# Group norm of a delta-rule head pair by sums and broadcast operands; one visit for the tiled output products, transposes six products later

## The chip, the cores and the metric

The kernel runs on one core of a Trainium2 chip, in one launch. The metric is the device time of that core in microseconds (us). The core's engines work side by side, each through its own list of instructions: TensorE (PE; its weight loads are shown apart as PEld), VectorE (DVE), ScalarE (ACT), GpSimd (POOL) and SyncE (SP, which here issues DMAs).

## The reference

One layer of a hybrid decoder trunk, for 512 tokens and 2048 channels, in float32:

```python
h = rms_norm(x, norm_g)
z = h @ w_in              # r, k, v, two low-rank inputs | gate | pool input | pool gate
r, k, v, wd, ad = token_shift_and_lerp(z[..., :3200])
decay = exp(-exp(-softplus(-(w0 + tanh(wd) @ w_up)) - 0.5))
a = sigmoid(a0 + ad @ a_up)
kk = normalized(k * k_k);  k = k * (1 + (a - 1) * k_a)
# per head of 64 channels, over time:
#   S = S * w_t + (S @ -kk_t) (kk_t * a_t)^T + v_t k_t^T ;  y_t = S @ r_t
y = wkv7_scan(r, decay, k, v, kk, a)
# head_group_norm: over the 64 channels of a head, at each position
yn = (y - mean(y)) * rsqrt(mean((y - mean(y))**2) + 64e-5)
y_rwkv = (yn * ln_w + ln_b + bonus) * silu(gate)
y_pool = causal_multiscale_pool(u) @ w_pool * pool_scale * silu(pool_gate)
x = x + concat(y_rwkv, y_pool) @ w_out
x = x + sigmoid(x @ w_pg + b_pg) * (p @ w_ple)
out = rms_norm(x, final_g)
```

The 16 heads are worked on in eight pairs, j = 0 to 7, of 128 channels each. The change concerns the last products of y and the group norm.

## The kernel before

**Dense products.** Each large matrix is split into a high and a low part, and a product is three matmuls (`mm3`: high by high, high by low, low by high) of 128 by 512 elements. The splits of the weights are made on the fly by ScalarE (line 132, the high part) and VectorE (line 133, the low part). A generator (`stream`) gives out the products with w_in for the coming pairs (names zr, zk, zv, zg), and those of the pool groups (zb, pp) and of the layer embedding (pple), in the order of a list. `pump(n)` issues the next n matmuls of it. These calls stand between the steps of the recurrence, so that TensorE has dense work while another engine makes the next operand.

**The recurrence of a pair** (`recur`) goes through eight chunks of 64 tokens. Per chunk TensorE has three small products in a chain: py (the state, sbd, by r and by k), which VectorE adds to mv for zs; pu (the inverted triangular factor x1 by zs), which ScalarE copies to uv; and ps (bkn by uv), from which VectorE makes the next state sbd. Six, nine and nine dense matmuls stand behind these three (`HC`). In chunk 0 `between()` issues the score products of the next pair (pm, by `scores`), whose results VectorE masks; during the later chunks VectorE also inverts the next pair's 32 by 32 blocks (`invert`, lines 657 and 661).

**The tiled products.** An output of a chunk has two parts: py, from the state, and the masked scores of the chunk (mt) by uv. The second are products with 128 rows, 64 columns and 64 moving columns, two heads per chunk; they add to the same PSUM tile, which holds four chunks. After chunk 3 and after chunk 7 TensorE makes eight such products in a row (in float32, two passes each, so 16 instructions), and ScalarE copies the tile into ysb with two instructions (line 827). A PSUM tile py has the tag "y" with two buffers, which it shares with half of the score tiles pm and with pv.

**The group norm** follows on VectorE: for each of the eight groups in a row of ysb (four times two heads) one bn_stats, one bn_aggr and one scaling (lines 842, 844, 851), and for all eight a reciprocal root by an integer guess and three Newton steps (`rsqrt`, lines 142 to 151).

**After the recurrence** `gather(j + 1)` prepares the next pair: the decay and rate products pu and pa, which ScalarE reads for sig and tha (lines 532 and 547); transposes of v (pv, copied to uv) and of the keys (pbk, two PSUM tiles, copied to bkn); H4 = 8 dense matmuls; the key norm (pss); H5 = 13 dense matmuls; then the pending `finish` of the pair before, which transposes the normed ysb into pyt, scales it on ScalarE (yo, line 860), adds the bonus and multiplies by the gate on VectorE (lines 861 and 862) and stores it; then HX = 13 dense matmuls; then the products of the blockwise inversion (pq, pmv, px), whose result ScalarE copies to x1 (line 745). For the last pair there is no `gather`; 40 dense matmuls (`HE`) stand before its `finish`. The PSUM tiles of tag "m" (pu, pa, pbk, pss, pyt, pq, pmv, px, pp) share three buffers.

**What sets the order.** TensorE's instructions keep the order in which the program emits them (`tc.keep_in_program_order`). The instructions of the other engines are put into an order at compile time by a planner, with priorities by their place in the program, and with `high_priority` and `issue_after` at the recurrence's critical ones. On the chip each engine follows its list.

Of the kernel before, what the change touches and what calls it, by code (L numbers as in the profile page):

```python
# [9 lines left out]
F32 = mybir.dt.float32  # L10
F32R = mybir.dt.float32r
I32 = mybir.dt.int32
AF = mybir.ActivationFunctionType
ALU = mybir.AluOpType

P = 128
T = 512
# [6 lines left out]
C = 64  # L24
NCH = T // C
# [9 lines left out]
def trunk_kernel(ctx: ExitStack, tc: tile.TileContext, x, p, norm_g, w_in, mu, w0, w_up, a0, a_up,  # L35
                 k_k, k_a, r_k, ln_w, ln_b, w_pool, pool_scale, w_out, w_ple, w_pg, b_pg, final_g, out):
    nc = tc.nc
    PSUM = bass.MemoryType.PSUM
    x, p, w_in, w_out, w_ple, w_pg = x[0], p[0, 0], w_in[0], w_out[0], w_ple[0], w_pg[0]
# [116 lines left out]
    def mm(*a, **k):  # L156
        i = nc.tensor.matmul(*a, **k)  # L157
        return tc.keep_in_program_order(i) if pin[0] else i

    def tr(*a):  # L160
        i = nc.tensor.transpose(*a)
        return tc.keep_in_program_order(i) if pin[0] else i
# [44 lines left out]
    for kind, nm, j in jobs:  # L207
# [7 lines left out]
        else:  # L215
            g, i = j // 4, j % 2
# [79 lines left out]
    for d in range(KT):  # L296
        xt_half(0, d)
        if d in WPOS:
            c = len(wl_)
# [41 lines left out]
    rw = s2a.enter_context(tc.tile_pool(name="rw", bufs=1))  # L341
    psS = s2a.enter_context(tc.tile_pool(name="psS", bufs=1, space=PSUM))
    psY = s2a.enter_context(tc.tile_pool(name="psY", bufs=2, space=PSUM))
# [148 lines left out]
    def pump(n):  # L492
        debt[0] += n
        while debt[0] > 0:
            c = next(big, None)
            if c is None:
                debt[0] = 0
                return
            debt[0] -= c
# [17 lines left out]
    H1, H2, H3, H4, H5, HE = 6, 12, 20, 8, 13, 40  # L517
# [36 lines left out]
    def prepare_key(j):  # L554
        k_ = need("k", j)
        kk = rw.tile([P, T], F32, name=f"kk{j}", tag="kk")
        nc.scalar.activation(kk, k_, AF.Square, scale=pc("k_k", j))
        kqh = rw.tile([P, T], F32R, name=f"kqh{j}", tag="t", bufs=4)
        kql = rw.tile([P, T], F32R, name=f"kql{j}", tag="t", bufs=4)
        split(kqh, kql, kk)  # L560
        kks[j] = (kk, kqh, kql)
# [116 lines left out]
    def gather(j):  # L678
        d = st_[j]
        bk, v_, mt = d.pop("bk"), d.pop("v_"), d["mt"]  # L680
        if j + 1 < NJ:
            prepare_key(j + 1)
            decay_and_rate(j + 1)

        uv = rw.tile([P, NCH, P], F32, name=f"uv{j}", tag="uv")
        ps = psY.tile([P, T], F32, name=f"pv{j}", tag="y")
        for tt in range(NT):
            tr(ps[:, tt * P:(tt + 1) * P], v_[:, tt * P:(tt + 1) * P], ident)
        pv = ps.rearrange("p (t c) -> p t c", c=P)
        nc.scalar.copy(uv[0:64, 0::2, :], pv[0:64])  # L690
        nc.scalar.copy(uv[64:128, 1::2, :], pv[64:128])


        bkn = rw.tile([P, NCH, P], F32, name=f"bkn{j}", tag="bkn")
        for hf in range(2):
            ps = psM.tile([P, T], F32, name=f"pbk{j}_{hf}", tag="m")
            for i in range(4):
                ch = 4 * hf + i
                tr(ps[:, i * P:(i + 1) * P], bk[:, ch // 2, 2 * (ch % 2):2 * (ch % 2) + 2, :], ident)
            nc.scalar.copy(bkn[:, 4 * hf:4 * hf + 4, :], ps.rearrange("p (c n) -> p c n", n=P))  # L700

        pump(H4)

        d.update(uv=uv, bkn=bkn)
        if j + 1 < NJ:
            norm_key(j + 1)
        pump(H5)
        if pending:
            pending.pop()()
        pump(HX)  # L710

        x1 = d["x1"]

        def units(fn):
            for u in range(8):
                for par in range(2):
                    fn(u, par, 64 * (1 - par))

        y1 = rw.tile([P, 8, 32], F32, name=f"y1{j}", tag="tm")

        with tc.issue_after(late[0].ins):
            for pb in (0, 64):
                yt = nc.vector.transpose(y1[pb:pb + 32], x1[pb:pb + 32, :, 0:32])
        if j + 1 < NJ:
            with tc.issue_after(yt.ins):
                scale_key(j + 1)
        ps3 = psM.tile([P, 8, 32], F32, name=f"pq2{j}", tag="m")
        units(lambda u, par, pb: mm(ps3[pb + 32:pb + 64, u, :],
                                                  mt[pb:pb + 32, par, u, 1 - par, 32:64],
                                                  y1[pb:pb + 32, u, :], start=True, stop=True,  # L730
                                                  tile_position=(pb, pb + 32)))
        q2t = rw.tile([P, 8, 32], F32, name=f"q2{j}", tag="xw")
        with tc.high_priority(offset=HP):
            for pb in (0, 64):
                nc.scalar.copy(q2t[pb + 32:pb + 64], ps3[pb + 32:pb + 64])
        psv = psM.tile([P, 8, C], F32, name=f"pmv{j}", tag="m")
        units(lambda u, par, pb: mm(psv[pb:pb + 64, u, :], mt[64 - pb:128 - pb, par, u, 1 - par, :],
                                    uv[64 - pb:128 - pb, 2 * (u // 2) + par, 64 * (u % 2):64 * (u % 2) + 64],
                                    start=True, stop=True))
        ps4 = psM.tile([P, 8, 32], F32, name=f"px2{j}", tag="m")  # L740
        units(lambda u, par, pb: mm(ps4[pb:pb + 32, u, :], q2t[pb + 32:pb + 64, u, :],
                                                  x1[pb + 32:pb + 64, u, 32:64], start=True, stop=True,
                                                  tile_position=(pb + 32, pb)))
        for pb in (0, 64):
            nc.scalar.copy(x1[pb:pb + 32, :, 32:64], ps4[pb:pb + 32])
        mv = rw.tile([P, 4, P], F32, name=f"mv{j}", tag="mv")
        nc.scalar.copy(zsp[0][64:128, :].rearrange("p (h t) -> p h t", h=2), psv[64:128, 0:2, :])
        nc.scalar.copy(mv.rearrange("p q (h t) -> p (q h) t", h=2), psv)
        d["mv"] = mv
        pump(2 * H1)  # L750


    def recur(j, work, between):
        d = st_.pop(j)
        pw, ar, mt, bv, uv, bkn, mv, x1 = (d[n_] for n_ in ("pw", "ar", "mt", "bv", "uv", "bkn", "mv", "x1"))
# [11 lines left out]


        ysb = rw.tile([P, NT, P], F32, name=f"ysb{j}", tag="t", bufs=4)
        py = None  # L770
        for ch in range(NCH):
            par, q = ch % 2, ch // 2
            pb = 64 * (1 - par)
# [1 line left out]
            pcc = pw[:, ch, C:C + 1]  # L775
            sl = slice((ch % 4) * P, (ch % 4 + 1) * P)
            if ch % 4 == 0:
                py = psY.tile([P, T], F32, name=f"py{j}_{ch}", tag="y")
            zs = zsp[par]
            if ch > 0:  # L780
                mm(py[:, sl], ar[:, q, 2 * par:2 * par + 2, :], cur, start=ch in (1, 4), stop=True,
                                 skip_group_check=True)
# [14 lines left out]
            if ch < NCH - 1:  # L797
# [12 lines left out]
                if ch < NCH - 2:  # L810
                    for h in range(2):
                        hc = slice(64 * h, 64 * h + 64)
                        nc.gpsimd.tensor_scalar(s0p[hc, :], nxt[hc, hc], pcn[hc], None, ALU.mult)  # L813
            if ch % 4 == 3:
                for qq in range(2):
                    for h in range(2):
                        for pr in range(2):
                            c_ = ch - 3 + 2 * qq + pr
                            yr = slice(64 * pr, 64 * pr + 64)
                            o_ = (2 * qq + pr) * P + 64 * h  # L820
                            mm(py[yr, o_:o_ + 64], mt[:, pr, 2 * (c_ // 2) + h, pr, :],
                                             uv[:, c_, 64 * h:64 * h + 64], start=False, stop=True,
                                             skip_group_check=True)
                py4 = py.rearrange("p (s c) -> p s c", c=P)
                for pr in range(2):
                    yr = slice(64 * pr, 64 * pr + 64)
                    nc.scalar.copy(ysb[yr, q - 1:q + 1, :], py4[yr, pr::2, :])
            step()
            if ch == 0:
                between()  # L830
# [4 lines left out]
            pass  # L835


        st = rw.tile([P, 8, 6], F32, name=f"st{j}", tag="st")
        mvr = rw.tile([P, 8, 2], F32, name=f"mvr{j}", tag="mvr")
        y8 = ysb.rearrange("p q (h c) -> p (q h) c", h=2)  # L840
        for i in range(8):
            nc.vector.bn_stats(st[:, i, :], y8[:, i, :])
        for i in range(8):
            nc.vector.bn_aggr(mvr[:, i, :], st[:, i, :])
        rs8 = rw.tile([P, 8, 1], F32, name=f"rs8{j}", tag="rs8")
        ve8 = rw.tile([P, 8, 1], F32, name=f"ve8{j}", tag="ve8")
        nc.vector.tensor_scalar(ve8, mvr[:, :, 1:2], 64e-5, None, ALU.add)
        nt8 = rw.tile([P, 8, 1], F32, name=f"nt8{j}", tag="nt8")
        rsqrt(rs8, ve8, nt8)
        for i in range(8):  # L850
            nc.vector.tensor_scalar(y8[:, i, :], y8[:, i, :], mvr[:, i, 0:1], rs8[:, i, :],
                                    ALU.subtract, ALU.mult)

        def finish():
            sg = need("g", j)
# [11 lines left out]
    HC, HT, HX = (6, 9, 9), 130, 13  # L867
# [13 lines left out]
    for _ in invert(0):  # L881
        pass
    pump(HT)
    gather(0)
    for j in range(NJ):
        def between():
# [291 lines left out]
```

## Time and profile before

| | |
|---|---|
| median of three runs | 1094.54 us (1093.39 to 1097.44) |
| the profiled execution | 1094.06 us, of which the profile's span is 1092.3 us |
| granted TensorE clock | 0.998 |
| busy: PE, PEld, DVE, ACT, POOL | 1067.4, 879.1, 707.9, 448.2, 74.4 us |
| tiled products (py<-uv,mt) | 256 instructions in 16 visits, 155.7 to 699.5 us |
| bn_stats, bn_aggr, scaling | 64 each; 11.0, 6.1, 15.4 us busy |

In the profile, a row of a timeline gives start, duration, engine, line, operation, and out<-in by the names of the program; a time in brackets is idle time before it, with what ended it. Rows merge equal neighbours (x16). A row of waits gives who waited for whom, then the total in us, how many times, and the longest. A row of a group gives shapes, count, busy time in us and mean ns of one, and then the idle time before them. L157 is the matmul helper, L161 the transpose helper, L132 and L133 the split of weights. Matmuls are pipelined, so that the start of the next one tells more than the duration.

### The profile page before, as it was taken

To read this page: it belongs to the slowest core of one execution; us is meant where nothing else is said; L and a number is where in the kernel's file an instruction comes from. 1 tells how busy PE (TensorE), PEld (TensorE's weight loads), DVE (VectorE), ACT (ScalarE), POOL (GpSimd) and SP (SyncE) were. 2 spreads that over 40 slices of the span, in tenths; PEclk is the share of its full clock that TensorE was granted. 3 is DMA by queue.
4 is the path that set the end of the run, shared out by engine and by line. 5 is a ranking of instruction groups with operands and counts; after the bars stand their busy time and mean duration, and the time that the engine had idled before them with its cause. 6 is when DMAs were issued, how large, how long until landed. Compare 5 with 4: busy or idle time off the path is not lost.

```text
span 1092.3 us, 17194 instructions
## 1 busy us (share of the span) xinstructions
PE 1067.4 (98%) x6060; PEld 879.1 (80%) x6060; DVE 707.9 (65%) x1835; ACT 448.2 (41%) x917; POOL 74.4 (7%) x180
## 2 busy tenths in 40 slices
PE   5999999999999999999999999999999999999996
PEld 4888878888888888787888788888888888888885
DVE  6687867878779679678886956454433424445366
ACT  7633534435335335353443344544222222233337
POOL 2100010110110110100101101000000000000000
PEclk9999999999999999999999999999999999999999
DMA  7433433332423333333334242774534438454534
GB/s 233 116 97 97 112 92 79 102 101 72 127 81 102 105 91 89 95 83 90 94 93 120 79 138 94 231 242 163 171 123 141 164 97 261 129 187 147 174 105 154
DMA packets 178485, 138.56 MB, mean 127 GB/s; under 512 B 34677, under 2 KB 139742, under 8 KB 178398
## 3 DMA queue, kind: packets, MB, share of 16 engines
q1 hardware_dynamic: 157694, 103.89, 32.2%
q10 hardware_dynamic: 20704, 33.56, 9.5%
q8 instruction: 48, 0.79, 0.3%
q14 instruction: 39, 0.32, 0.1%
HBM read 118.02 MB, written 18.87 MB: 125 GB/s over the span
## 4 chain that ended last, share of the span: by engine, by line
PE 88%; DVE 5%; DMA 3%; ACT 2%; issue 1%; SPq 0%; ACTq 0%; DVEq 0%
PE acc_o L157 16%; PE acc_g L157 16%; PE zb L157 15%; PE zv L157 8%; PE zr L157 7%; PE zg L157 7%; PE zk L157 6%; DMA n<-nd 2%; PE py L157 2%; PE pple L157 2%; PE pu L157 2%; PE pm L157 1%; PE pp L157 1%; PE ps L157 1%; PE pmv L157 1%
## 5 line engine op out<-in xcount | busy, mean ns | idle before, releaser
L133 DVE TENSOR_TENSOR wlo_g<-raw_g,whi_g 128x512 fp32r<-128x512 f32 x84 | 56.9, 683 | 78.7 <-ACT whi_g L132 78.5
L157 PE MATMUL zb<-hhi,whi_b 128*128 128x512 f32 x256 | 106.3, 415 | 0.0
L133 DVE TENSOR_TENSOR wlo_o<-raw_o,whi_o 128x512 fp32r<-128x512 f32 x64 | 43.9, 690 | 92.3 <-ACT whi_o L132 92.2
L157 PE MATMUL zb<-hhi,wlo_b 128*128 128x512 f32 x256 | 100.5, 393 | 0.0
L157 PE MATMUL acc_o<-whi_o,ylo 128*128 128x512 f32 x256 | 100.2, 391 | 0.0
L157 PE MATMUL acc_o<-whi_o,yhi 128*128 128x512 f32 x256 | 99.9, 390 | 0.0
L157 PE MATMUL zb<-hlo,whi_b 128*128 128x512 f32 x256 | 99.8, 390 | 0.0
L157 PE MATMUL acc_o<-wlo_o,yhi 128*128 128x512 f32 x256 | 99.7, 389 | 0.0
L132 ACT CAST whi_g<-raw_g 128x512 fp32r<-128x512 f32 x84 | 51.9, 620 | 105.5 <-PE acc_g L157 60.3
L157 PE MATMUL acc_g<-whi_g,x2hi 128*128 128x512 f32 x208 | 81.2, 391 | 0.0
L157 PE MATMUL acc_g<-wlo_g,x2hi 128*128 128x512 f32 x208 | 81.0, 389 | 0.0
L157 PE MATMUL acc_g<-whi_g,x2lo 128*128 128x512 f32 x208 | 80.6, 389 | 0.0
L132 ACT CAST whi_o<-raw_o 128x512 fp32r<-128x512 f32 x64 | 39.9, 623 | 97.8 <-PE acc_o L157 97.8
L813 POOL TENSOR_SCALAR s0p<-sbd,pw 64x64 f32<-64x64 f32 x96 | 56.7, 590 | 338.5 <-DVE sbd L806 253.7
L132 ACT CAST whi_b<-raw_b 128x512 fp32r<-128x512 f32 x64 | 39.7, 620 | 87.1 <-PE zv L157 34.9
L133 DVE TENSOR_TENSOR wlo_b<-raw_b,whi_b 128x512 fp32r<-128x512 f32 x64 | 43.7, 684 | 34.2 <-ACT whi_b L132 33.0
L157 PEld LDWEIGHTS zb<-hhi,wlo_b 128*128 128x128 f32 x256 | 48.0, 188 | 11.0
L661 DVE TENSOR_TENSOR xw<-xw,tm 128x60 f32<-128x60 f32 (+24 forms) x248 | 51.9, 209 | 6.8
L157 PEld LDWEIGHTS acc_o<-wlo_o,yhi 128*128 128x128 f32 x256 | 48.1, 188 | 10.0
L157 PEld LDWEIGHTS acc_o<-whi_o,ylo 128*128 128x128 f32 x256 | 48.1, 188 | 9.9
L157 PEld LDWEIGHTS acc_o<-whi_o,yhi 128*128 128x128 f32 x256 | 48.1, 188 | 9.6
L157 PEld LDWEIGHTS zb<-hhi,whi_b 128*128 128x128 f32 x256 | 48.3, 189 | 8.4
(285 smaller groups left out, 2546.8 us busy)
## 6 DMA issues: line engine op xcount, KB each, us to landing
raw_b<-in_w_in_dram SPq DMA_DIRECT2D x64, 256.0 KB
raw_o<-in_w_out_dram SPq DMA_DIRECT2D x64, 256.0 KB
raw_g<-in_w_pg_dram SPq DMA_DIRECT2D x64, 256.0 KB
raw_k<-in_w_in_dram SPq DMA_DIRECT2D x32, 256.0 KB
raw_r<-in_w_in_dram SPq DMA_DIRECT2D x32, 256.0 KB
raw_v<-in_w_in_dram SPq DMA_DIRECT2D x32, 256.0 KB
raw_g<-in_w_in_dram SPq DMA_DIRECT2D x32, 256.0 KB
n<-nd SPq DMA_DIRECT2D x16, 256.0 KB
```

The lines of the kernel that those rows point to most:

```text
L132: nc.scalar.copy(hi, raw)
L133: nc.vector.tensor_tensor(lo, raw, hi.bitcast(F32), ALU.subtract)
L157: i = nc.tensor.matmul(*a, **k)
L661: nc.vector.tensor_tensor(xw[:, 0:n_, s + 1:32], xw[:, 0:n_, s + 1:32], tm[:, 0:n_, 0:w_], ALU.add)
L813: nc.gpsimd.tensor_scalar(s0p[hc, :], nxt[hc, hc], pcn[hc], None, ALU.mult)
```

## The change

Three things, in one edit.

The tiled products after chunk 3 are left out there; after chunk 7 one visit makes those of all eight chunks, first chunks 0 to 3 and then 4 to 7, and after each half come its two copies into ysb. Both PSUM tiles py live until then.

The group norm takes a sum over the 64 channels of all eight groups at once, scales it to the negative mean, adds it to ysb with a broadcast operand, squares the result on ScalarE into a new tile (in the buffer of mv), sums the squares on VectorE, scales and adds epsilon, takes the same `rsqrt`, and multiplies ysb by it with a broadcast operand. The 24 instructions by group are gone.

In `gather`, six dense matmuls move from behind the transposes of the pair before to ahead of them: 19 and 7 in place of 13 and 13.

```diff
-        pump(H5)
+        pump(H5 + 6)
         if pending:
             pending.pop()()
-        pump(HX)
+        pump(HX - 6)
...
-        py = None
+        pys = {}
...
             if ch % 4 == 0:
-                py = psY.tile([P, T], F32, name=f"py{j}_{ch}", tag="y")
+                pys[ch // 4] = psY.tile([P, T], F32, name=f"py{j}_{ch}", tag="y")
+            py = pys[ch // 4]
...
-            if ch % 4 == 3:
-                for qq in range(2):
-                    for h in range(2):
-                        for pr in range(2):
-                            c_ = ch - 3 + 2 * qq + pr
...
+            if ch == NCH - 1:
+                for c0 in range(0, NCH, 4):
+                    py = pys[c0 // 4]
+                    for qq in range(2):
+                        for h in range(2):
+                            for pr in range(2):
+                                c_ = c0 + 2 * qq + pr
+                                yr = slice(64 * pr, 64 * pr + 64)
+                                o_ = (2 * qq + pr) * P + 64 * h
+                                mm(py[yr, o_:o_ + 64], mt[:, pr, 2 * (c_ // 2) + h, pr, :],
+                                   uv[:, c_, 64 * h:64 * h + 64], start=False, stop=True, skip_group_check=True)
+                    py4 = py.rearrange("p (s c) -> p s c", c=P)
+                    for pr in range(2):
+                        yr = slice(64 * pr, 64 * pr + 64)
+                        nc.scalar.copy(ysb[yr, c0 // 2:c0 // 2 + 2, :], py4[yr, pr::2, :])
...
-        for i in range(8):
-            nc.vector.bn_stats(st[:, i, :], y8[:, i, :])
-        for i in range(8):
-            nc.vector.bn_aggr(mvr[:, i, :], st[:, i, :])
...
+        nc.vector.tensor_reduce(mn8, y8, mybir.AxisListType.X, ALU.add)
+        nc.vector.tensor_scalar(mn8, mn8, -1.0 / C, None, ALU.mult)
+        nc.vector.tensor_tensor(y8, y8, mn8.to_broadcast([P, 8, C]), ALU.add)
+        ysq = rw.tile([P, 8, C], F32, name=f"ysq{j}", tag="mv")
+        nc.scalar.activation(ysq, y8, AF.Square)
+        ve8 = rw.tile([P, 8, 1], F32, name=f"ve8{j}", tag="ve8")
+        nc.vector.tensor_reduce(ve8, ysq, mybir.AxisListType.X, ALU.add)
...
-        nc.vector.tensor_scalar(ve8, mvr[:, :, 1:2], 64e-5, None, ALU.add)
+        nc.vector.tensor_scalar(ve8, ve8, 1.0 / C, 64e-5, ALU.mult, ALU.add)
...
         rsqrt(rs8, ve8, nt8)
-        for i in range(8):
-            nc.vector.tensor_scalar(y8[:, i, :], y8[:, i, :], mvr[:, i, 0:1], rs8[:, i, :],
-                                    ALU.subtract, ALU.mult)
+        nc.vector.tensor_tensor(y8, y8, rs8.to_broadcast([P, 8, C]), ALU.mult)
```

More of the change, by code (lines that the diff above doesn't have):

```diff
@@ L813, in recur @@
                         nc.gpsimd.tensor_scalar(s0p[hc, :], nxt[hc, hc], pcn[hc], None, ALU.mult)
-            if ch % 4 == 3:
-                for qq in range(2):
-                    for h in range(2):
-                        for pr in range(2):
-                            c_ = ch - 3 + 2 * qq + pr
[L819 to L827, printed above, removed]
+            if ch == NCH - 1:
[13 more added lines that the diff above has]
+                        nc.scalar.copy(ysb[yr, c0 // 2:c0 // 2 + 2, :], py4[yr, pr::2, :])
             step()
@@ L835, in recur @@
             pass
-        st = rw.tile([P, 8, 6], F32, name=f"st{j}", tag="st")
-        mvr = rw.tile([P, 8, 2], F32, name=f"mvr{j}", tag="mvr")
         y8 = ysb.rearrange("p q (h c) -> p (q h) c", h=2)
-        for i in range(8):
-            nc.vector.bn_stats(st[:, i, :], y8[:, i, :])
-        for i in range(8):
-            nc.vector.bn_aggr(mvr[:, i, :], st[:, i, :])
+        mn8 = rw.tile([P, 8, 1], F32, name=f"mn8{j}", tag="mn8")
+        nc.vector.tensor_reduce(mn8, y8, mybir.AxisListType.X, ALU.add)
[5 more added lines that the diff above has]
+        nc.vector.tensor_reduce(ve8, ysq, mybir.AxisListType.X, ALU.add)
         rs8 = rw.tile([P, 8, 1], F32, name=f"rs8{j}", tag="rs8")
-        ve8 = rw.tile([P, 8, 1], F32, name=f"ve8{j}", tag="ve8")
-        nc.vector.tensor_scalar(ve8, mvr[:, :, 1:2], 64e-5, None, ALU.add)
+        nc.vector.tensor_scalar(ve8, ve8, 1.0 / C, 64e-5, ALU.mult, ALU.add)
         nt8 = rw.tile([P, 8, 1], F32, name=f"nt8{j}", tag="nt8")
         rsqrt(rs8, ve8, nt8)
-        for i in range(8):
-            nc.vector.tensor_scalar(y8[:, i, :], y8[:, i, :], mvr[:, i, 0:1], rs8[:, i, :],
-                                    ALU.subtract, ALU.mult)
+        nc.vector.tensor_tensor(y8, y8, rs8.to_broadcast([P, 8, C]), ALU.mult)
         def finish():
```

## The prediction

> **What bounds the kernel now.** I read the page first, then the view of waits for TensorE's weight loads (each matmul is preceded by one, so a late operand shows there), then the timelines round one head pair.
>
> ```profile
> span 1092.3 us, 17194 instructions
> PE 1067.4 (98%) x6060; PEld 879.1 (80%) x6060; DVE 707.9 (65%) x1835; ACT 448.2 (41%) x917; POOL 74.4 (7%) x180
> PE 88%; DVE 5%; DMA 3%; ACT 2%; issue 1%; SPq 0%; ACTq 0%; DVEq 0%
> ```
>
> TensorE has work for 98% of the span and makes 88% of the chain that ended last. A gain must therefore take time out of TensorE's own stream, or remove one of its waits; work taken from VectorE (65%) or ScalarE (41%) counts only where TensorE stands still for it. The waits that bear on the head pairs are few:
>
> ```profile
> PEld py L157 <- DVE sbd L806: 5.9, 9, 1.0
> PEld pu L157 <- DVE zs L784: 3.4, 6, 0.9
> PEld py L157 <- issue: 2.9, 8, 0.4
> PEld pu L157 <- ACT x L745: 2.0, 2, 1.4
> PEld pbk L161 <- ACT sig L532: 0.4, 2, 0.3
> ```
>
> The columns are total, times and longest. The recurrence waits 11.3 us in all for VectorE and ScalarE (5.9 + 3.4 + 2.0), in 17 places out of some 180 steps. No row has the transposes of the group-normed outputs (pyt) as the waiting side: in eight pairs they never waited. Moving them later thus removes no wait that exists; it can only make room for a normalization that ends later.
>
> **What the joined visit saves.** The change leaves out the visit of tiled products after chunk 3 and puts its 16 instructions (eight products, each two passes) at the head of the visit after chunk 7. TensorE's timeline has a step without a visit and the step with one:
>
> ```profile
> 223.13 0.38 PE L157 MATMUL ps<-uv,bkn 128*128 128x128 f32 x2
> 223.27 0.47 PE L157 MATMUL zk<-hhi,whi_k 128*128 128x512 f32 x1
> 223.59 0.39 PE L157 MATMUL zk<-hlo,whi_k 128*128 128x512 f32 x1
> ...
> 229.35 0.38 PE L157 MATMUL ps<-uv,bkn 128*128 128x128 f32 x2
> 229.66 0.69 PE L157 MATMUL py<-uv,mt 128*64 128x64 f32 x16
> 230.27 0.50 PE L157 MATMUL zk<-hhi,whi_k 128*128 128x512 f32 x1
> 230.61 0.39 PE L157 MATMUL zk<-hlo,whi_k 128*128 128x512 f32 x1
> ```
>
> From the start of ps to the start of the second dense product it is 223.59 - 223.13 = 0.46 us without a visit and 230.61 - 229.35 = 1.26 us with one, so the visit costs 0.80 us. The products alone are cheaper:
>
> ```profile
> L157 PE MATMUL py<-uv,mt x256: 222/222/271, 155.7 to 699.5; 128*64 128x64 f32 x128
> 255.10 0.69 PE L157 MATMUL py<-uv,mt 128*64 128x64 f32 x16
> ```
>
> Sixteen take 0.69 us and one lasts 0.222, so sixteen starts spread over 0.69 - 0.22 = 0.47 us; that is what the second sixteen add to a visit that is already open. The remaining 0.33 us is for going into the 128*64 form and out again, and the change pays it once per pair instead of twice. 0.80 - 0.47 = 0.33 us, times 8 pairs, is **2.6 us saved**. The bounds: 0, if the second sixteen cost a change of their own (they write another PSUM bank, which no visit here does), and 8 x 0.80 = 6.4 us, if they cost nothing. I take 2.6, since every visit shows the same spread.
>
> **What moving the transposes costs.** The same products are issued, six of them before the transposes instead of after.
>
> ```profile
> 225.81 1.39 PE zk L157 x6
> ```
>
> Six dense products are 1.39 us. With the 0.47 us of the longer visit the transposes stand 1.86 us later after the visit's start; TensorE loses nothing by the exchange. What is queued behind them: ScalarE's scaling (yo), two VectorE products and the store, which feeds the output projection much later, and the PSUM buffer that pyt holds, wanted again by the inversion's products, now seven dense products behind it, 1.6 us, where yo ends 1.4 us behind its start (266.27 + 0.78 - 265.63, rows below): at least 0.2 us to spare. I cost it at 0; were yo held by 0.5 us, behind one weight cast, it would be 0.3 us for seven pairs, 2 us.
>
> **What the normalization costs.** From the groups by shape:
>
> ```profile
> L842 DVE BATCH_NORM_STATS2 st<-ysb 128x6 f32<-128x64 f32 x64 | 11.0, 215 | 4.3 <-ACT ysb L827 4.3
> L844 DVE BATCH_NORM_AGGREGATE mvr<-st 128x2 f32<-128x6 f32 x64 | 6.1, 155 | 0.0
> L851 DVE TENSOR_SCALAR ysb<-ysb,mvr,rs 128x64 f32<-128x64 f32 x64 | 15.4, 309 | 0.1
> L623 DVE TENSOR_TENSOR mt<-pm,msk 128x512 f32<-128x512 f32 x32 | 19.9, 681 | 0.7 <-PE pm L157 0.6
> L591 DVE TENSOR_SCALAR kp<-tha,dprm 128x512 f32<-128x512 f32 x8 | 4.3, 539 | 0.0
> L534 DVE TENSOR_TENSOR_SCAN sig<-seg,sig 128x512 f32<-128x512 f32 x8 | 9.8, 1220 | 0.0
> L557 ACT ACTIVATE kk<-sk,prm 128x512 f32<-128x512 f32 x8 | 5.8, 724 | 9.7 <-DVE sk L370 7.3 <-ACT uv L794 2.3
> ```
>
> Removed from VectorE per pair: (11.0 + 6.1 + 15.4) / 8 = 4.1 us. Added: two products with a broadcast operand at 0.68 (L623 is such a one), two reductions, and a small scalar operation of 0.17. No reduction of this size is in the trace; it lies between 0.54 (L591, one operand) and 1.22 us (the scan), and I take 0.69, as for any other pass over 512 columns. Sum 2.9 us, so VectorE does 1.2 us less per pair, of which half the statistics, (11.0 + 6.1) / 16 = 1.1 us, leaves the middle of the recurrence. ScalarE gets a squaring pass, 0.72 us (L557 is a square of that size), which includes no load of a function table: L557 runs between Tanh and Exp, and the trace's only table loads before 1065 us are these:
>
> ```profile
> L72 ACT ACT_TABLE_LOAD x1 | 1.3, 1283 | 0.8 <-PEq L1167 0.8
> L378 ACT ACT_TABLE_LOAD x1 | 1.3, 1283 | 0.0
> ```
>
> All of that is beside TensorE. The question is whether the normalization still ends before the transposes, and whom the square holds up. The pair that ended its recurrence at 255 us:
>
> ```profile
> 255.86 0.75 ACT L827 COPY ysb<-py 64x256 f32<-64x256 f32 x2 [0.96 <-PE py L157]
> 257.76 0.17 DVE L143 TENSOR_SCALAR rs<-ve 128x8 int32<-128x8 int32 x1
> 258.56 0.69 ACT L369 ACTIVATE sv<-zv,dprm 128x512 f32<-128x512 f32 x1
> 258.82 0.60 PE L161 MATMUL pv<-ident,sv 128*128 128x128 f32 x4
> 259.15 0.68 ACT L532 ACTIVATE sig<-pu,dprm 128x512 f32<-128x512 f32 x1
> 259.26 1.28 PE L161 MATMUL pbk<-ident,bk 128*128 128x128 f32 x8
> 262.84 0.16 DVE L151 SCALAR_TENSOR_TENSOR rs<-nt,rs 128x8 f32<-128x8 f32 x1
> 265.16 0.30 DVE L851 TENSOR_SCALAR ysb<-ysb,mvr,rs 128x64 f32<-128x64 f32 x1
> 265.63 0.60 PE L161 MATMUL pyt<-ident,ysb 128*128 128x128 f32 x4
> 266.27 0.78 ACT L860 ACTIVATE yo<-pyt,dprm 128x512 f32<-128x512 f32 x1 [1.47 <-PE pyt L161]
> ```
>
> Call the visit's start (255.10) zero. Before, the copies end at 1.51, the last scaling at 10.36 and the transposes begin at 10.53: 0.17 us to spare. After, four copies follow each other; the first half is copied while the second half is multiplied, so they end 0.75 later, at 2.26. Then reduction 0.69, mean 0.2, subtraction 0.69, square 0.72, reduction 0.69, scaling 0.2 and a handover of 0.1 twice: 5.65. The root takes 263.00 - 257.76 = 5.24 with the other work that VectorE puts between its small steps: 10.9. The product with the root ends at 11.6, and the transposes begin at 10.53 + 1.86 = 12.39. **It ends in time, with 0.8 us left, so 0.** Without work in between, it would be 3 us earlier. The last pair has a fixed 40 products before its transposes, not changed; there I allow one wait of up to 1 us.
>
> The square comes to ScalarE at about 3.95, which is 259.05 on that clock, and sig is wanted from 259.15. It is emitted earlier in the program, so I expect it first, and sig then ends at about 260.6 instead of 259.83. The second half of pbk needs the buffer that sig reads; it already waits here (0.4 us in two of six pairs), and stands 0.47 later itself. That makes 0.3 us more in the pairs that wait today, little in the others: **0.5 us lost** over six pairs. Bounds: -0.4 (sig goes first, both waits vanish) and 6 x 0.7 = 4.2 us.
>
> Against it stands the VectorE time freed in the recurrence. Of the 11.3 us of waits I give back **0.5 us**; between 2 us gained and 2 us lost, since every added or removed instruction changes the order in which the planner lines up the others on these two engines.
>
> Sum: -2.6 + 0.5 - 0.5 = -2.6 us on the profiled execution's 1094.06 us (span 1092.3 and 1.8 around it): 1091.5. That execution lies 0.5 us under the median of the runs, 1094.54, so the median comes to **1092.0 us**.
>
> **The rivals.**
>
> Given back: the square, or a pushed copy, stands ahead of sig or of the key's copies in most pairs, and the saved 2.6 us is lost again at 0.45 us in each of six: 1092.0 + 2.7 = 1094.7. For it speaks that pbk has no slack in two pairs; against it, that the other four never waited.
>
> Slower, by the chain of the normalization: it now crosses from VectorE to ScalarE and back, and each of them works through its instructions one by one. If the square waits behind sv, sig and tha (2.0 us) and the second reduction behind the scan (1.2 us), the 11.6 above becomes 14.8, against the transposes at 12.39; TensorE would stand 2.4 us in each of up to seven pairs. It decides from 12.39 on; halfway, with 1.2 us in eight pairs, it gives 1092.0 + 9.6 = 1101.6. For it: only 0.17 us were left before. Against it: while VectorE waits it can do the work that otherwise lies between the root's steps.
>
> Faster: the 1.1 us less of statistics per recurrence clears most VectorE waits after the middle, and the total falls by 3 us more: 1089. For it: waits on sbd and zs are 9.3 us; against: most of them lie before the middle, when the masks of the next pair are multiplied, and the statistics only come after it.
>
> No PSUM buffer: both py tiles now live until the end, and they are the only two buffers of their tag, which pv needs next. pv begins at 258.82 + 0.47, the first tile's copies end at 255.10 + 1.51 = 256.61: 2.7 us to spare. If ScalarE was late by 3.2 us in seven pairs, it would cost 0.5 us each, 1095.5. The Trainium skill, Perfetto Trace Analysis, Optimization Strategy, says that consistent bubbles on the saturated engine can mean that PSUM has no room for the next tile; by that rule pv would show a gap in every pair. The trace before has no such gap and cannot show this one.
>
> That the change does nothing on TensorE (the second sixteen cost a full visit) gives 1094.5, the zero bound above.
>
> **How the numbers follow.** 0.54 for the forecast, with its own range 1089.5 to 1094; 0.12 for given back, 0.05 for PSUM and 0.05 for no effect (all three 1094 to 1097); 0.10 for faster (1086 to 1089.5); 0.14 for slower (1097 to 1108). The range 1088 to 1098 leaves out about 0.05 below and 0.12 above. A change of 0.5%, 5.5 us, is what a measurement of this kernel can tell from none: faster than 1089.1 gets 0.09, slower than 1100.0 gets 0.10, between them 0.81.
>
> **What would show it.** Right: 32 tiled instructions in one group per pair, about 1.16 us long, none after chunk 3; 0.33 us less per pair; no row of TensorE waiting in pyt; reductions near 0.69 us. Wrong: rows of pyt waiting for VectorE, of pbk waiting for sig in more than two pairs, of pv waiting for ysb, or a second sixteen that cost over 0.6 us.

## The result, and the profile after

The changed kernel takes 1145.88 us (median of 4 runs, 1144.68 to 1147.79) where the kernel before, on the same chip, takes 1094.61 us: a ratio of 1.0466, with a 95% interval of 1.0444 to 1.0487. That is 51 us slower, where 2.6 us faster was forecast, and outside the range of 1088 to 1098. The profiled execution took 1147.79 us, the slowest of the four. Two of the runs further below had one execution each at a far lower granted clock (0.753 and 0.559), and their medians leave it out.

The page of the changed kernel says this of the span, the busy times and the chain:

```profile
span 1146.1 us, 17044 instructions
PE 1076.2 (94%) x6060; PEld 886.9 (77%) x6060; DVE 701.4 (61%) x1683; ACT 452.8 (40%) x925; POOL 70.0 (6%) x180
PE 81%; DVE 10%; DMA 4%; ACT 2%; issue 2%; SPq 0%; ACTq 0%; DVEq 0%
```

TensorE has the same 6060 matmuls, VectorE is busy 6.5 us less (707.9 to 701.4), and yet VectorE now has 10% of the chain that ended last instead of 5%. The waits of TensorE's weight loads and of its matmuls (total, times, longest) say where:

```profile
PEld pyt L161 <- issue: 30.9, 4, 8.6
PEld pyt L161 <- ACT dh L137: 8.7, 1, 8.7
PEld py L157 <- DVE sbd L807: 7.8, 9, 2.3
PEld pyt L161 <- DVE ysb L853: 5.2, 1, 5.2
PEld pbk L161 <- ACT sig L532: 1.8, 2, 0.9
```

```profile
PE pyt L161 <- DVE ysb L853: 35.5, 5, 8.3
PE pyt L161 <- DVE sw L418: 7.0, 1, 7.0
```

The transposes pyt, which never waited before, stand still for 42.5 us (35.5 + 7.0) in six places: pairs 0 to 5. The timeline of the first of them follows, TensorE first, and then what VectorE did in the meantime, from the root's first step (L143) to the last product of the norm (L853):

```profile
192.92 0.39 PE L157 MATMUL zb<-hhi,wlo_b 128*128 128x512 f32 x1
201.55 1.09 PE L161 MATMUL pyt<-ident,ysb 128*128 128x128 f32 x4 [8.24 <-DVE ysb L853]
202.29 0.78 PE L157 MATMUL zb<-hhi,whi_b 128*128 128x512 f32 x1
202.86 0.63 PE L157 MATMUL zb<-hlo,whi_b 128*128 128x512 f32 x1
203.29 0.63 PE L157 MATMUL zb<-hhi,wlo_b 128*128 128x512 f32 x1
```

```profile
189.86 0.16 DVE L143 TENSOR_SCALAR rs<-ve 128x8 int32<-128x8 int32 x1
189.93 0.69 DVE L592 TENSOR_TENSOR kp<-kp,sk 128x512 f32<-128x512 f32 x1
190.53 0.17 DVE L144 TENSOR_SCALAR ve<-ve 128x8 f32<-128x8 f32 x1
190.60 0.68 DVE L568 TENSOR_SCALAR kk<-pss 128x512 f32<-128x512 f32 x1
191.20 0.16 DVE L149 TENSOR_TENSOR nt<-rs,ve 128x8 f32<-128x8 f32 x1
...
193.60 0.15 DVE L149 TENSOR_TENSOR nt<-rs,ve 128x8 f32<-128x8 f32 x1
193.67 3.34 DVE L572 RECIPROCAL kk<-kk 128x512 f32<-128x512 f32 x1
196.94 0.62 DVE L133 TENSOR_TENSOR wlo_g<-raw_g,whi_g 128x512 fp32r<-128x512 f32 x1
197.48 0.15 DVE L150 TENSOR_TENSOR nt<-nt,rs 128x8 f32<-128x8 f32 x1
197.55 0.74 DVE L573 SCALAR_TENSOR_TENSOR kk<-sk,prm,kk 128x512 f32<-128x512 f32 x1
198.21 0.15 DVE L151 SCALAR_TENSOR_TENSOR rs<-nt,rs 128x8 f32<-128x8 f32 x1
...
200.12 0.68 DVE L599 TENSOR_TENSOR kk<-kk,tha 128x512 f32<-128x512 f32 x1
200.72 0.68 DVE L853 TENSOR_TENSOR ysb<-ysb,rs 128x512 f32<-128x512 f32 x1
```

VectorE is never idle here. Between any two of the root's eleven small steps (0.15 to 0.17 us each) its list has another operation, mostly one of 0.4 to 0.7 us over 512 columns, and once the key's reciprocal of 3.34 us. They belong to the next pairs or to the weights of coming products (L133), and the transposes do not need them. Counted in this trace from the end of the copies to the norm's last instruction, 17 to 22 other instructions with 13.4 to 15.2 us of work stand in the norm of pairs 0 to 5; in the kernel before it was 5 to 8 with 3.2 to 5.7 us. The norm ends 16.0 to 17.7 us after the copies; before, it was 7.8 to 9.4. Pairs 6 and 7, behind which there is less left to prepare, have 5 and 2 others and wait 0 and 0.3 us.

The norm is late before its root begins, too. In the same pair a cast for the next key stands between the copies on ScalarE, and among the sums on VectorE stands work on sig, a scan above all:

```profile
181.78 0.74 ACT L829 COPY ysb<-py 64x256 f32<-64x256 f32 x2 [0.24 <-PE py L157]
182.55 0.62 ACT L137 CAST kqh<-kk 128x512 fp32r<-128x512 f32 x1
183.20 0.75 ACT L829 COPY ysb<-py 64x256 f32<-64x256 f32 x2
```

```profile
184.90 0.69 DVE L844 TENSOR_TENSOR ysb<-ysb,mn 128x512 f32<-128x512 f32 x1
...
186.41 1.23 DVE L534 TENSOR_TENSOR_SCAN sig<-seg,sig 128x512 f32<-128x512 f32 x1
187.55 0.66 DVE L848 TENSOR_REDUCE ve<-ysq 128x8 f32<-128x512 f32 x1
188.12 0.54 DVE L591 TENSOR_SCALAR kp<-tha,dprm 128x512 f32<-128x512 f32 x1
188.58 0.17 DVE L850 TENSOR_SCALAR ve<-ve 128x8 f32<-128x8 f32 x1
```

Counted from the visit's start, the copies of pairs 0 to 5 end at 2.6 to 2.9 us (1.5 to 1.8 before), the root begins at 7.1 to 8.8 us and ends at 17.7 to 19.2, and the norm ends at 18.9 to 20.4.

The gap has a tail: the dense products after it are 0.43 us apart (202.86 to 203.29) where 0.23 us is usual. Stretches of that time, with TensorE's granted clock in the column after the engines':

```profile
192.90:201.50 8.60, 0.41 (x2) 0.00 (x0) 8.60 (x18) 0.62 (x1) 0.00 (x0) 0.67 0.23 65
201.50:205.50 4.00, 3.95 (x12) 3.31 (x13) 3.26 (x6) 1.29 (x2) 0.00 (x0) 0.50 0.07 16
205.50:209.50 4.00, 4.00 (x103) 3.23 (x102) 0.00 (x0) 2.13 (x6) 0.40 (x1) 0.93 0.20 72
```

For 4 us after the gap the granted clock is 0.50. The change without the Newton steps (one of the experiments below) has the same 6060 matmuls in the same order, no wait in pyt, and the span of the kernel before, 1092.3 us. Compared with it from start to start of neighbouring matmuls, the steps into pyt are 43.7 us longer, those in the 9 us behind them 11.4 us (2.3 in the transposes, 8.9 in the slowed dense products), and all others together 1.3 us shorter. That is the 53.8 us by which the span grew (1092.3 to 1146.1).

### The profile page after: what moved, and what is told of

Its sections match the earlier page's. It is cut to its first block, busy times and chain, and to the rows that moved or that the text cites. A ratio compares the mean times of both kernels' runs of the same rounds, so it can differ in the third digit from the quotient of the medians.

```text
span 1146.1 us, 17044 instructions
## 1 busy us (share of the span) xinstructions
PE 1076.2 (94%) x6060; PEld 886.9 (77%) x6060; DVE 701.4 (61%) x1683; ACT 452.8 (40%) x925; POOL 70.0 (6%) x180
## 4 chain that ended last, share of the span: by engine, by line
PE 81%; DVE 10%; DMA 4%; ACT 2%; issue 2%; SPq 0%; ACTq 0%; DVEq 0%
PE acc_o L157 15%; PE acc_g L157 15%; PE zb L157 12%; PE zv L157 7%; PE zr L157 7%; PE zg L157 6%; PE zk L157 6%; DMA n<-nd 2%; PE py L157 2%; DVE kk L572 2%; PE pple L157 1%; PE pu L157 1%; PE pm L157 1%; PE pp L157 1%; PE ps L157 1%
## 5 line engine op out<-in xcount | busy, mean ns | idle before, releaser
L133 DVE TENSOR_TENSOR wlo_g<-raw_g,whi_g 128x512 fp32r<-128x512 f32 x84 | 56.9, 684 | 102.4 <-ACT whi_g L132 102.3
L157 PE MATMUL zb<-hhi,whi_b 128*128 128x512 f32 x256 | 109.0, 426 | 0.0
L157 PE MATMUL zb<-hlo,whi_b 128*128 128x512 f32 x256 | 102.2, 399 | 0.0
L133 DVE TENSOR_TENSOR wlo_o<-raw_o,whi_o 128x512 fp32r<-128x512 f32 x64 | 43.9, 690 | 91.2 <-ACT whi_o L132 91.2
L814 POOL TENSOR_SCALAR s0p<-sbd,pw 64x64 f32<-64x64 f32 x96 | 52.8, 550 | 336.8 <-DVE sbd L807 257.3
L133 DVE TENSOR_TENSOR wlo_b<-raw_b,whi_b 128x512 fp32r<-128x512 f32 x64 | 43.8, 686 | 35.9 <-ACT whi_b L132 34.6
L157 PEld LDWEIGHTS zb<-hhi,wlo_b 128*128 128x128 f32 x256 | 49.6, 194 | 11.6
L157 PEld LDWEIGHTS zb<-hlo,whi_b 128*128 128x128 f32 x256 | 49.9, 195 | 8.5
```

The lines of the kernel that those rows point to most:

```text
L133: nc.vector.tensor_tensor(lo, raw, hi.bitcast(F32), ALU.subtract)
```

## The experiments

Three theories were set against each other. A: other work in VectorE's list, drawn in between the norm's small steps, makes the norm late. B: the crossing to ScalarE for the square does. C: the copies, forecast to end 0.75 us later, do; measured, they end 0.8 to 1.4 us later.

**The joined visit alone.** The kernel before, with this part of the change only:

```diff
-            if ch % 4 == 3:
+            if ch == NCH - 1:
+                for c0 in range(0, NCH, 4):
```

> The kernel before with the joined visit alone (bn_stats norm, 13 and 13 dense products round the transposes). Theory A, other work listed between the root's small steps on VectorE makes the norm late: this program's list has 11 to 15 others in the norm of pairs 0 to 5 (6 to 11 us of work) where before had 5 to 8 (3 to 5.4 us), so the transposes wait 2 to 7 us in each, some 23 us in all, less 2.6 us for the visit, plus about 3 us at a lower TensorE clock after the gaps: near 1117 us. Theory B, the crossing to ScalarE for the square makes it late: there is none here, so 1092 us. Theory C, the copies that end 0.75 us later are late by themselves: six waits of about 0.5 us, 1095 us.

Measured: 1114.01 us, ratio 1.0176 (1.0148 to 1.0203). The old statistics run on VectorE and nothing crosses to ScalarE, and still the transposes wait:

```profile
PE pyt L161 <- DVE ysb L853: 14.0, 8, 5.3
```

In pairs 0 to 5 the norm has 11 to 15 others (6.7 to 11.6 us), and the two pairs whose list has the reciprocal inside (1 and 2) wait 4.2 and 5.4 us, the other four 0.6 to 1.9. A visit that ends half a microsecond later, and copies that end 0.8 to 1.4 us later, were enough to double the foreign work in the norm. B cannot be the cause here, and C's price of 0.5 us a pair is far too small. The late copies do not cost much by themselves: a run below has them as late, with the other work held back, and no transposes wait.

**The new norm alone.** The kernel before with the sums, the square and the broadcast products, two visits and 13 and 13 dense products:

```diff
-        for i in range(8):
-            nc.vector.bn_stats(st[:, i, :], y8[:, i, :])
+        nc.vector.tensor_reduce(mn8, y8, mybir.AxisListType.X, ALU.add)
...
+        nc.scalar.activation(ysq, y8, AF.Square)
```

> The kernel before with the new group norm alone (two visits, 13 and 13 dense products). Theory A: its list has 15 to 18 others in the norm of pairs 0 to 5 (11.6 to 13.1 us of work), so each of the six waits 6 to 9 us, 44 us in all, plus about 9 us at a lower clock: 1140 to 1150 us, as slow as the whole change. Theory B: the same sign, but only the square's handover, 1 to 2 us for each pair: 1105 us. Theory C: 1094 us, since the copies are as early as before.

Measured: 1149.07 us, ratio 1.0492 (1.0468 to 1.0516), so as slow as the whole change within the two intervals, as A had it. Its transposes wait 5.4 to 8.8 us in each of pairs 0 to 5, with 15 to 18 others in the norm. The copies end as early as before (1.5 to 1.8 us after the visit's start), so C falls.

**The moved dense products alone.**

```diff
-        pump(H5)
+        pump(H5 + 6)
...
-        pump(HX)
+        pump(HX - 6)
```

> The kernel before with the six dense products moved ahead of the transposes alone. Its list on VectorE has the same work in the norm as before. All theories: no change, 1094.5 us within 2 us. A rival by which the later transposes themselves cost something (the PSUM buffer of pyt, held 1.4 us longer): 1096 to 1100 us.

Measured: 1094.42 us, ratio 0.9996 (0.9982 to 1.0010). That is no change, as all expected: in its trace no transposes wait and none of the inversion's products wait for their buffer.

**The whole change with a rule of order.** The instructions are the same; the next key's scaling and the preparation of the pair after next may stand only behind the norm:

```diff
-        nc.vector.tensor_tensor(y8, y8, rs8.to_broadcast([P, 8, C]), ALU.mult)
+        normed[0] = nc.vector.tensor_tensor(y8, y8, rs8.to_broadcast([P, 8, C]), ALU.mult)
...
-            with tc.issue_after(yt.ins):
+            with tc.issue_after(yt.ins), tc.issue_after((normed[0] or yt).ins):
                 scale_key(j + 1)
...
-            prepare(j + 1)
+            with tc.issue_after((normed[0] or late[0]).ins):
+                prepare(j + 1)
```

> The whole change, with one ordering rule more: the scaling of the next key (with the reciprocal of 3.35 us) and the preparation of the pair after next may stand in VectorE's list only behind the norm's last instruction. Same instructions otherwise. Theory A: 5 to 8 others remain in the norm (3 to 4.8 us), the transposes do not wait, and the saved 2.6 us shows: 1092 us (1090 to 1095). Theory B: the crossing remains, so most of the 51 us remains: above 1130 us. Theory C: likewise, since the copies end as late as in the change.

Measured: 1095.45 us, ratio 1.0006 (0.9992 to 1.0020). The 51 us are gone, with the square on ScalarE and the late copies still there: theory A. The same stretch of VectorE's timeline as above:

```profile
188.45 0.17 DVE L143 TENSOR_SCALAR rs<-ve 128x8 int32<-128x8 int32 x1
188.66 0.17 DVE L144 TENSOR_SCALAR ve<-ve 128x8 f32<-128x8 f32 x1
188.86 0.17 DVE L149 TENSOR_TENSOR nt<-rs,ve 128x8 f32<-128x8 f32 x1
189.06 0.17 DVE L150 TENSOR_TENSOR nt<-nt,rs 128x8 f32<-128x8 f32 x1
...
192.40 0.68 DVE L853 TENSOR_TENSOR ysb<-ysb,rs 128x512 f32<-128x512 f32 x1
...
194.26 3.33 DVE L572 RECIPROCAL kk<-kk 128x512 f32<-128x512 f32 x1
```

The root begins 1.4 us earlier and the norm ends 8.3 us earlier (200.72 to 192.40), and the reciprocal comes behind it. But the expected 1092 us was missed by 3 us. Some waits grew or are new:

```profile
PEld pm L157 <- DVE bk L600: 3.7, 2, 1.9
PEld pbk L161 <- ACT sig L532: 1.8, 2, 0.9
PEld ps L157 <- ACT uv L795: 1.5, 2, 0.8
```

The next scores wait 3.7 us in two pairs for bk (0.7 before), which the preparation makes from the scaled key; both are held here, and this run does not tell them apart. And pbk waits 1.4 us more for sig. That wait is 0.4 us with the joined visit alone or with the square on VectorE, 0.6 us with the new norm alone, and 1.8 us in every run that has both the joined visit and the square on ScalarE.

**The joined visit with the old norm and the same rule of order.** 

> The kernel before with the joined visit and, as in the run before, the next key's scaling and the preparation of the pair after next held behind the norm's last instruction in VectorE's list; bn_stats norm, 13 and 13 dense products. Theory A: 4 to 6 others in the norm (2.6 to 4.3 us of work, less than before had), so the transposes do not wait and the 2.6 us of the joined visits shows: 1092.4 us. If holding the preparation makes the next pair's scores late, as it did with the new norm (3.7 us of weight loads of pm waiting for bk), 1094 to 1096 us. If the joined visit saves nothing, 1095 us without any such wait.

Measured: 1094.82 us, ratio 0.9997 (0.9987 to 1.0007). The second of the three cases came in: no waits in pyt, but 4.5 us of pm waiting for bk. Holding work back cures the norm and bills the next pair.

**The whole change without Newton steps.** The root is left at its guess, so this kernel computes less:

```diff
-        rsqrt(rs8, ve8, nt8)
+        rsqrt(rs8, ve8, nt8, 0)
```

> The whole change without the three Newton steps of the norm's root: nine of its eleven small instructions are left out, so the root is the integer guess alone, good to some per cent. Nothing is held. Theory A: each small step draws one other instruction into the list, so with nine steps gone only 5 to 8 others (3.4 to 4.7 us) remain in the norm of pairs 0 to 5 and no transposes wait: 1091 to 1094 us. A rival by which it is the norm's late start and not its steps that lets the next pair's work in: most of the waits remain, above 1125 us.

Measured: 1092.03 us, ratio 0.9980 (0.9968 to 0.9992). Nothing was held, and the root starts as late as in the change (7.1 to 8.8 us after the visit's start); with nine of the root's eleven steps out, 5 to 8 others are left in the norm and no transposes wait. The nine instructions take 1.5 us a pair by their own durations (9 x 0.165), and their removal takes 54 us out. Their own time can't account for that; the places beside them, which the list fills, can. The rival, that the late start alone lets the next pairs' work in, falls.

**The square on VectorE.**

```diff
-        nc.scalar.activation(ysq, y8, AF.Square)
+        nc.vector.tensor_tensor(ysq, y8, y8, ALU.mult)
```

> The whole change with the square made on VectorE (ysb by ysb) in place of ScalarE, so that the norm never leaves VectorE. Theory A: its list still has 17 to 21 others in the norm of pairs 0 to 5 (12.3 to 13.7 us), so the six waits stay: 1138 to 1147 us. Theory B, the crossing to ScalarE: it is gone, so 1092 to 1100 us.

Measured: 1145.38 us, ratio 1.0460 (1.0439 to 1.0480): within the intervals the same as the whole change, so the crossing to ScalarE has no measurable part in the loss. Theory B falls.

**The whole change with its transposes later still.**

```diff
         pump(H5 + 6)
-        if pending:
-            pending.pop()()
         pump(HX - 6)
...
         d["mv"] = mv
         pump(2 * H1)
+        if pending:
+            pending.pop()()
```

> The whole change with the transposes moved further, behind the inversion's products and 12 dense products after them (some 7 us later than in the change). Theory A: the norm still ends 16 to 18 us after its copies, which is about where the transposes now stand, so at most 1 us of wait in each of six pairs and no low clock: 1092 to 1100 us. A rival by which the work inside the norm delays the inversion and the scores of the next pair as well: TensorE waits in pq, px or pm instead, above 1105 us.

Measured: 1095.13 us, ratio 1.0010 (0.9998 to 1.0021). The norm still ends 16 to 18.5 us after its copies, with 17 to 23 others in it; the waits in pyt shrink to 0 to 2.0 us a pair, two of them twice what was expected. Of TensorE's other waits in the recurrence and the inversion, that of pm for bk is longer than in the change, by 0.7 us (as long as in the kernel before), and no other by more than 0.4 us. So nearly all of the 51 us is gone with the norm as crowded as ever: it costs time where TensorE comes for its result too early.

**The joined visit alone, with the transposes moved as far.** The old statistics stay, and nothing is held:

> The kernel before with the joined visit and the transposes moved behind the inversion's products and 12 dense products after them; bn_stats norm, nothing held in VectorE's list. Theory A: 11 to 16 others stand in the norm (6 to 12 us), as with the joined visit alone, so it ends 10 to 15 us after the copies; the transposes come some 18 us after them and never wait, and nothing is held that the scores need: the 2.6 us of the joined visit shows, 1092.4 us. If moving the transposes so far has a cost of its own (VectorE's two products on yo fall among the next pair's preparation), 1095 us or more.

Measured: 1090.33 us, ratio 0.9960 (0.9944 to 0.9976). This beats both kernels. In its trace the norm ends 10.2 to 15.5 us after the copies and the transposes have 1.9 us or more to spare in pairs 0 to 5; pyt has no row among TensorE's waits. The gain of 4.5 us is 2 us above the joined visit's 2.6; its weight loads wait 4.5 us for sbd (5.9 before) and not at all for x1 (2.0 before). That these follow from the change and not from a list that happens to fall better was not tested.

**The whole change with late transposes and only the key's scaling held.**

> The whole change with the transposes moved as in the run before, and only the next key's scaling (with the reciprocal) held behind the norm's last instruction; the preparation of the pair after next is free. Theory A: about 17 to 22 others stand in the norm (10 to 12 us), it ends some 13 to 15 us after the copies, no wait in pyt: 1092 to 1094 us, the waits of pbk for sig (1.4 us) being the difference from the run before.

Measured: 1095.98 us, ratio 1.0009 (0.9995 to 1.0023), so 2 us above what was expected. No transposes wait apart from the last pair (0.3 us), but pm waits 3.2 us for bk and pbk 1.8 us for sig. Holding the key's scaling alone, behind a norm that ends 13.3 to 15.0 us after the copies, is thus enough to make bk late. Its profiled execution took 1092.83 us, the fastest of its runs, so the trace does not show the median's last 3 us; they stay open.

## Why the prediction was wrong

**The joined visit** was right. The timeline after shows the 32 instructions in one group:

```profile
181.05 1.15 PE L157 MATMUL py<-uv,mt 128*64 128x64 f32 x32
182.13 0.50 PE L157 MATMUL zv<-hhi,whi_v 128*128 128x512 f32 x1
```

This is the next dense product behind the visit of 255.10 before:

```profile
255.72 0.50 PE L157 MATMUL zv<-hhi,whi_v 128*128 128x512 f32 x1
```

From the visit's start to the next dense product it is 1.08 us; before, 255.72 - 255.10 = 0.62. The second sixteen cost 0.46 us (0.47 predicted), so 0.34 us per pair is saved. In the two runs where no transposes wait and nothing is held back, the kernel is faster by 2.9 us (without the Newton steps) and by 4.5 (the joined visit with late transposes); other waits differ there too, so these are no clean measure of the visit.

**The moved products** were right too: 0, and no product of the inversion that waited for yo.

**The durations** were right: the two reductions take 0.686 and 0.674 us (0.69 taken), the broadcast products 0.692 and 0.683 (0.68), and the square 0.630 (0.72). The wait of pbk for sig rose from 0.4 to 1.8 us; 0.5 us was predicted, and the 1.4 us lie inside the stated bounds.

**The step that failed** is the sum that ends in "It ends in time, with 0.8 us left, so 0", and in it, above all, "the root takes 5.24 with the other work that VectorE puts between its small steps". The sum put the norm's end at 11.6 us after the visit's start; it came at 18.9 to 20.4.

| after the visit's start, us | predicted | measured, pairs 0 to 5 |
|---|---|---|
| the copies end | 2.26 | 2.6 to 2.9 |
| the root begins | 5.65 | 7.1 to 8.8 |
| the root lasts | 5.24 | 9.8 to 11.1 |
| the norm ends | 11.6 | 18.9 to 20.4 |

The sum allowed no other work between the copies and the root, and there were four to seven instructions of it. This alone would have used up the 0.8 us: with a root of 5.24 us the norm would still have ended at 13.0 us or later, behind the 12.39 of the transposes. The larger part came in the root, 4.6 to 5.9 us. The prediction took the other work in the root of one pair before (4.3 us, in six places) for a constant of the root. It is not: in that pair the first five steps stood next to each other, and the filling began behind them:

```profile
258.38 0.17 DVE L150 TENSOR_TENSOR nt<-nt,rs 128x8 f32<-128x8 f32 x1
258.58 0.17 DVE L151 SCALAR_TENSOR_TENSOR rs<-nt,rs 128x8 f32<-128x8 f32 x1
258.69 0.69 DVE L133 TENSOR_TENSOR wlo_b<-raw_b,whi_b 128x512 fp32r<-128x512 f32 x1
```

The list has room beside nearly every one of the root's steps, and how much goes in depends on what is ready by then. That the joined visit alone, with the old statistics and copies 0.8 to 1.4 us later, already has 11 to 15 others shows that the start matters; that the change without Newton steps has 5 to 8 with the same late start shows that each small step matters. Which costs the planner had in mind when it filled the places can't be read from a trace and stays open.

**The rival on the other side**, "slower, by the chain of the normalization", named the right place, the right wait and the right point of decision (12.39 us after the visit's start), but a wrong mechanism: a square queued behind sv, sig and tha. In the trace the square of pair 0 stands behind sig alone and begins 0.1 us after the subtraction's end, and with the square on VectorE the time is the same. Its second half, the second reduction behind the scan, did come in pairs 0, 2 and 4 (187.55 behind 186.41 above); it is one part of the late start of the root. The rival's worst price, 2.4 us a pair, was a third of the 5.0 to 8.5 us that came. What spoke "against it", that VectorE would do the other work while it waits for ScalarE, was backwards: with more time there was more other work ready, not less left. The 0.8 us to spare was worked out for one pair with the list of the kernel before, which was not the list that the changed program would have.

**The tail** was not in the prediction at all: a gap on TensorE was priced at its own length. The steps behind the gaps took 11.4 us more.

**The faster rival**, less work on VectorE in the recurrence, did not come. The three waits that the prediction added up to 11.3 us are 10.8 us now: py waits 7.8 us for sbd (5.9 before), pu 3.0 for zs (3.4 before) and not at all for x1 (2.0 before). The 0.5 us that were given back are thus met, but by luck, since the terms moved in opposite directions.

## What to carry to other kernels

Where a planner sets an engine's order, a chain of many short dependent instructions is not as long as their sum: each of them is a place where other ready work can be put in front of the next, and the same chain can take up to twice the time when it starts a little later. Before such a chain is moved or rewritten, read the list of the new program, not the old one's, and count what stands between its steps; here fewer steps, a rule that held the other work back, or a consumer that comes later each took nearly all of the loss away. Joining small products of another shape into one visit is a real but small gain, and here it showed only where the transposes did not wait and nothing was held back.

## What the runs showed of the hardware

After the change, the six gaps of 5.0 to 8.5 us on TensorE are each followed by 3.0 to 5.1 us, counted from the transposes' start, at half the granted clock (0.50), in which dense products stand 0.43 us apart instead of 0.23; the 11.4 us behind the gaps are a fifth of the loss. The Trainium skill, TensorE: Matmul & The Clock Gate, section "HAM oscillation — how this bites in real kernels", gives idle gaps beyond some 3.4 us as what drops the clock to half. The trace agrees for the gaps of 5 to 8 us here. With the joined visit alone, whose two long gaps are 4.2 and 5.4 us and whose others are under 2 us, the clock over the run was 0.991, against 0.977 with six long gaps and 0.998 with none. There the gap of 1.9 us was followed by a stretch at 0.50 as well: its transposes waited again, so that 3.5 us lay between two dense products. Breaks of 2.3 to 2.8 us between dense products, in three other pairs of that run, were not.
